# Three blocks on one core: retention's values computed tokens-major from x, half-width convolution taps that run on, and block 2's outputs in another order

## The chip, the cores and the metric

The kernel runs on 1 core of one Trainium2 chip. The metric is the device time of one execution in microseconds (us), the median of several runs; lower is better. A profile of one execution gives the span and the instructions of each engine: PE (TensorE matmuls, with PEld its weight loads), DVE (VectorE), ACT (ScalarE), POOL (GpSimd) and SP (SyncE, which only issues transfers).

## The reference, cut to what is touched

The program is three transformer-like blocks over 1024 tokens of width 1024. Only the second is changed:

```python
proj = u @ w_in[l]                       # 1024 x 7168
conv_a, conv_bp, conv_gate = ...         # 1024 columns each
q, k, v = ...                            # 4 heads x 256 columns each
ret_gate = proj[..., o6:]
a = conv_a * jax.nn.sigmoid(conv_bp)
a = _causal_depthwise_conv(a, conv_w[l], conv_b[l])        # 31 taps
a = jax.nn.silu(_layernorm(a, conv_ln_g[l], conv_ln_b[l]))
y_conv = (a @ conv_pw[l]) * jax.nn.silu(conv_gate)
q = _rotary(q); k = _rotary(k) * (RET_QK_DIM ** -0.5)
r = _retention_chunkwise(q, k, v)                          # chunks of 128 tokens
r = _head_groupnorm(r, ret_gn_g[l], ret_gn_b[l])
y_ret = r * jax.nn.silu(ret_gate)
y = jnp.concatenate([y_conv, y_ret], axis=-1) @ w_out[l]
h = h + gate * y
```

## The kernel before

All is float32. A product of full accuracy is made of three TensorE products: each operand is split into a high and a low part (`split`, L159 on ACT for the high part and L160 on DVE, or on POOL, for the low part), and high x high, high x low and low x high are added up in PSUM. `mm3` (L234 to L236) does that with a weight tile stationary and 512 tokens moving, so its result is channels-major: 128 channels on the partitions, tokens along the row.

Block 2's first stage, the *mixed stage*, goes over a list `plan` of groups. A group is 256 output columns of `w_in` (two tiles of 128) for all 1024 tokens. It is computed with seven half-size products in place of eight (`Mixed`, L638 to L640: 7 x 4 x 3 = 84 products of 512 columns), of which POOL makes the combinations of the weights (L607 to L615) and, from the third group on, also the seven low parts; ACT and DVE gather the results from PSUM (L650 to L659). There are 24 groups: 4 gates, 8 for the convolution's input (`conv`), and 4 each for q, k and v. q and k are turned by the rotary tables on DVE and POOL (L1210 to L1215). A group of v comes out channels-major, though the retention wants tokens on the partitions, so `values` transposes it on PE (16 transposes a group, L1223) and stores it in DRAM.

Behind the products stands a background queue, `core.bg`. `worked` adds `rate` x products / 16 to a counter and `tick` takes one job for each whole unit. In the mixed stage the jobs are the 31 taps of the convolution, on DVE, one instruction of 128x1024 for each tap and channel tile, with a sum of 1024 columns in PSUM (two banks). At the end of the stage `core.drain()` runs what is left.

Then comes the retention: 16 steps (4 heads x 4 pairs of chunks), each a chain of small products over PE, DVE, ACT and POOL, with `fill(n)` between its links: n pieces of the products for `conv_gate`, whose results go to DRAM. The layer norm of the convolution (sum, mean, `ln_center`, `ln_rstd`, `ln_scale`) is the background work there.

Last the outputs: the normed convolution is split into X; `w_pw` products give the convolution's output G; then `w_out` times G, while the retention's output is read back and split into X; and `block2_out` adds `w_out` times X. The tables of block 3 (`s5_tables`, 22 jobs, most of them DVE and POOL work) are the background there, at rate 1.5.

PSUM has eight banks. Before, `mm` has three, the taps' sum two in the mixed stage (where `mm` isn't used), `pa` two, `pb` two and `pc` one.

Of the kernel before, what the change touches and what calls it, by code (L numbers as in the profile page):

```python
# [1 line left out]

# [10 lines left out]
ALU = mybir.AluOpType  # L13
# [19 lines left out]
RQ = 6  # L33
RT = 8
# [3 lines left out]
RB = 13  # L38
# [19 lines left out]
class Core:  # L58


    def __init__(self, ctx, tc, ins):
# [12 lines left out]

        self.lent = ctx.enter_context(ExitStack())
        self.banks()
# [19 lines left out]
    def banks(self, name="psum_mm"):  # L96

        self.lent.close()
        self.psm = self.lent.enter_context(self.tc.tile_pool(name=name, bufs=1, space=PSUM))
# [967 lines left out]
def block2_input(core, X, h, rrb, scratch):  # L1067
# [13 lines left out]
             for i in range(RH) for n, kind in enumerate(("q", "k", "v"))]  # L1081
    order = plan[:2] + conv[:2]
    for i in range(2, KT):
        order += conv[i:i + 1] + heads[2 * i - 4:2 * i - 2]
# [48 lines left out]
def block2(core, X, scratch, tabs, keep, after):  # L1133
# [7 lines left out]
    with ExitStack() as st:  # L1141
        cvp = st.enter_context(tc.tile_pool(name="b2_conv", bufs=1, reuse_waits="tile"))
        A = [cvp.tile([P, PAD + S], F32, tag=f"a{c}", name=f"cv_{c}") for c in range(KT)]

        def tap(c, j, state):
            def run():
                if j == 0:
                    state["acc"] = core.psum("acc", (P, S))
                    nc.vector.tensor_scalar(state["acc"], A[c][:, :S], core.vec("conv_w_2", c),
                                            core.vec("conv_b_2", c), ALU.mult, ALU.add)  # L1150
                    return
                out = A[c][:, PAD:] if j == CW - 1 else state["acc"]
                nc.vector.scalar_tensor_tensor(out, A[c][:, j:j + S], core.vec("conv_w_2", j * KT + c), state["acc"],  # L1153
                                               ALU.mult, ALU.add)
            return run
# [3 lines left out]
        core.banks("psum_conv")  # L1159
        with tc.tile_pool(name="b2_mix", bufs=1, reuse_waits="tile") as pool:  # L1160
# [5 lines left out]
            turns = []  # L1166
# [4 lines left out]
            def gather(f, name):  # L1171
# [16 lines left out]
                elif name == "a22":  # L1188
                    {"conv": conv, "q": turned, "k": turned, "v": values}[kind](kind, i, g, u)
                if name in ("a12", "s2"):  # L1190
                    while turns and len(turns) > (2 if name == "a12" else 0):
                        turns.pop(0)()
# [5 lines left out]
            def conv(_, c, a, b):  # L1198
# [4 lines left out]
                core.bg += [tap(c, j, state) for j in range(CW)]  # L1203
# [14 lines left out]

            def values(_, i, a, b):
                def turn(k, y, half):  # L1220
                    pt = core.psum("pc")
                    for j in range(4):
                        nc.tensor.transpose(pt[:, j * P:(j + 1) * P], y[:, (half * 4 + j) * P:(half * 4 + j + 1) * P], core.ident)  # L1223
                    t = temp()
                    nc.scalar.activation(t, pt, AF.Copy)
                    nc.sync.dma_start(heads["v"][i, :, half * 4:half * 4 + 4, k], t.rearrange("p (b c) -> p b c", b=4))
                turns.extend([lambda k=k, y=y, half=half: turn(k, y, half) for k, y in enumerate((a, b)) for half in range(2)])
# [26 lines left out]
            while turns:  # L1254
                turns.pop(0)()
            core.paced = None
            core.drain()
        scratch["mixed"].close()
        core.banks()
        with tc.tile_pool(name="b2_ret", bufs=1, reuse_waits="tile") as pool:  # L1260
            ln = {}

            def ln_sum(c):
                if c == 0:
                    return
                if c == 1:
                    ln["acc"] = pool.tile([P, S], F32, tag="lnacc", name="ln_acc")
                nc.gpsimd.tensor_tensor(ln["acc"], A[0][:, PAD:] if c == 1 else ln["acc"], A[c][:, PAD:], ALU.add)

            def ln_mean():  # L1270
                ln["mu"] = pool.tile([P, S], F32, tag="lnmu", name="ln_mu")
# [5 lines left out]
            def ln_center(c):  # L1277
                a = A[c][:, PAD:]
                nc.vector.tensor_tensor(a, a, ln["mu"], ALU.subtract)
                if c == 0:  # L1280
                    ln["var"] = pool.tile([P, S], F32, tag="lnacc", name="ln_var")
                    nc.scalar.activation(ln["var"], a, AF.Square)
                else:
                    sq = core.raw()
                    nc.scalar.activation(sq, a, AF.Square)
                    nc.gpsimd.tensor_tensor(ln["var"], ln["var"], sq, ALU.add)

            def ln_rstd():
                ln["r"] = core.rsqrt(core.token_sums(ln["var"], pool), pool)

            def ln_rows():
                ln["r"] = core.rows(ln["r"], pool)

            def ln_spread():
                ln["rb"] = core.over_partitions(ln["r"], pool, tag="lnmu")
# [6 lines left out]
            om = pool.tile([P, P], F32, tag="onesm", name="onesm")  # L1302
            nc.vector.memset(om, 1.0 / D)
            done = list(ready)

            def ln_ready(c):
                ln_sum(c)

# [3 lines left out]
            core.bg += pause * 4 + [ln_mean] + pause * 4 + [lambda c=c: ln_center(c) for c in range(KT)]  # L1312
            core.bg += pause * 8 + [ln_rstd] + pause * 2 + [ln_rows] + pause * 2 + [ln_spread] + [lambda c=c: ln_scale(c) for c in range(KT)]
# [7 lines left out]
            def conv_gates():  # L1321
                nxt = core.weights(w_in, 0, KT, 2 * D)
                for c in range(KT):
                    w = nxt
                    for half in range(2):
                        ps = core.psum("mm")
                        for k in range(KT):
# [1292 lines left out]
```

## Time and profile before

| | before |
|---|---|
| median of 3 runs | 3751.67 us (3744.95 to 3754.52) |
| the profiled execution | 3755.68 us, its span 3753.9 us |
| busy share of the span | PE 92%, DVE 68%, POOL 48%, ACT 42% |
| mean granted clock of TensorE | 0.956 |

In the profiled execution the mixed stage goes from 1538 to 2126 us, the retention to about 2345, the two outputs that the change swaps to about 2552, and `block2_out` to 2655. A busy PE in these views is modelled: each product is shown with its whole way through the array, so that products that follow each other overlap, and the distance from start to start is what one costs in a row of them.

### The profile page before, as it was taken

Reading aid. Unit: us, or ns where it says so; the run is one execution under the profiler, and the core shown is the slowest. Engines: PE = TensorE matmul, PEld = TensorE weight load, DVE = VectorE, ACT = ScalarE, POOL = GpSimd, SP = SyncE. Lnnn points to the kernel's source line nnn. Section 1 sums busy time; section 2 is a strip of 40 time slices with the busy share of each in tenths; the row PEclk is TensorE's granted clock in tenths of the full one; section 3 lists DMA queues with packets and bytes.
Section 4 is the critical chain, followed back from the end, with each engine's and each line's share of the span. In section 5 each row is a group of like instructions: output and inputs, shape, how many; then the busy total and the mean of one; then the engine's idle time right before and its main releaser. Section 6 shows DMA issues by size and latency. Waiting matters only on the chain. (4 is left out here: it accounts for less than half of the span.)

```text
span 3753.9 us, 45804 instructions
## 1 busy us (share of the span) xinstructions
PE 3448.4 (92%) x16540; PEld 2779.9 (74%) x16540; DVE 2553.3 (68%) x3211; ACT 1571.2 (42%) x2731; POOL 1806.0 (48%) x1690
## 2 busy tenths in 40 slices
PE   8999989899998999898889989889899689899998
PEld 7878777677776778576667778668677468677876
DVE  7888897777766555768989664874556365755644
ACT  5666674433334444532223343214443124653334
POOL 2343343456554534567677653436428884331122
PEclk9999999999999999899989999999899899899999
DMA  4101026333325323322122454465443135225513
GB/s 142 37 30 37 28 69 234 109 95 107 107 93 184 114 76 120 111 73 79 62 73 68 141 160 124 126 195 185 128 152 108 57 89 159 88 84 191 178 48 110
DMA packets 431134, 409.85 MB, mean 109 GB/s; under 512 B 34059, under 2 KB 364347, under 8 KB 430907
## 3 DMA queue, kind: packets, MB, share of 16 engines
q1 hardware_dynamic: 396164, 330.27, 28.5%
q0 software_dynamic: 21088, 68.19, 5.0%
q10 hardware_dynamic: 13655, 8.46, 0.8%
q8 instruction: 131, 2.15, 0.2%
q14 instruction: 96, 0.79, 0.1%
HBM read 284.80 MB, written 122.03 MB: 108 GB/s over the span
## 5 line engine op out<-in xcount | busy, mean ns | idle before, releaser
L159 ACT ACTIVATE whi<-raw 128x512 fp32r<-128x512 f32 (+3 forms) x610 | 431.1, 737 | 787.8 <-PE pb L639 214.4
L160 DVE TENSOR_TENSOR wlo<-raw,whi 128x512 fp32r<-128x512 f32 (+3 forms) x456 | 545.9, 1219 | 227.5 <-ACT whi L159 223.9
L234 PE MATMUL mm<-x,whi 128*128 128x512 f32 x1152 | 462.4, 402 | 9.3 <-ACT whi L159 3.9
L236 PE MATMUL mm<-x,wlo 128*128 128x512 f32 x1152 | 458.0, 399 | 6.0 <-DVE wlo L160 6.0
L235 PE MATMUL mm<-x,whi 128*128 128x512 f32 x1152 | 460.4, 400 | 0.5 <-DVE x L163 0.2
L493 POOL TENSOR_TENSOR s<-s,f 128x127 f32<-128x127 f32 (+1 forms) x192 | 194.4, 1020 | 293.6 <-DVE f L492 190.9
L1153 DVE SCALAR_TENSOR_TENSOR acc<-cv,par,acc 128x1024 f32<-128x1024 f32 x232 | 298.1, 1285 | 4.3
L638 PE MATMUL pa<-x,whi 128*128 128x512 f32 x648 | 262.2, 405 | 24.2 <-ACT u L659 16.8
L234 PE MATMUL mm<-yc,whi 128*128 128x512 f32 (+1 forms) x656 | 267.1, 407 | 7.4 <-ACT whi L159 4.3
L235 PE MATMUL mm<-yc,whi 128*128 128x512 f32 (+1 forms) x656 | 266.9, 407 | 6.0 <-DVE yc L160 5.9
L640 PE MATMUL pa<-x,wlo 128*128 128x512 f32 x648 | 260.7, 403 | 8.0 <-DVE wlo L160 7.9
L236 PE MATMUL mm<-yc,wlo 128*128 128x512 f32 (+1 forms) x656 | 265.3, 405 | 1.6 <-DVE wlo L160 1.5
L639 PE MATMUL pa<-x,whi 128*128 128x512 f32 x648 | 260.5, 402 | 6.8 <-DVE x L160 6.8
L640 PE MATMUL pb<-x,wlo 128*128 128x512 f32 x576 | 234.0, 411 | 32.0 <-POOL wlo L160 22.4
L638 PE MATMUL pb<-x,whi 128*128 128x512 f32 x576 | 237.2, 412 | 27.6 <-ACT whi L159 8.8
L234 PEld LDWEIGHTS mm<-x,whi 128*128 128x128 f32 x1152 | 219.7, 191 | 56.0 <-ACT whi L159 4.7
L236 PEld LDWEIGHTS mm<-x,wlo 128*128 128x128 f32 x1152 | 218.9, 190 | 52.8 <-DVE wlo L160 7.5
L160 POOL TENSOR_TENSOR wlo<-raw,whi 128x512 fp32r<-128x512 f32 x154 | 215.4, 1418 | 82.6 <-ACT whi L159 82.5
L235 PEld LDWEIGHTS mm<-x,whi 128*128 128x128 f32 x1152 | 219.5, 191 | 45.2 <-DVE x L163 0.6
L639 PE MATMUL pb<-x,whi 128*128 128x512 f32 x576 | 234.6, 407 | 3.2 <-DVE x L160 3.1
L492 DVE TENSOR_TENSOR_SCAN f<-f 128x128 f32<-128x128 f32 (+1 forms) x192 | 196.0, 1035 | 39.7 <-ACT f L485 38.6
L607 POOL TENSOR_TENSOR raw<-raw 128x512 f32<-128x512 f32 x58 | 79.9, 1377 | 246.9 <-DMA raw<-in_ffn_w_in_dram 119.7
(599 smaller groups left out, 8443.4 us busy)
## 6 DMA issues: line engine op xcount, KB each, us to landing
raw<-in_w_in_dram SPq DMA_DIRECT2D x96, 512.0 KB
raw<-in_ffn_w_in_dram SPq DMA_DIRECT2D x44, 512.0 KB
raw<-in_w_out_dram SPq DMA_DIRECT2D x32, 512.0 KB
g<-g_dram SPq DMA_DIRECT2D x56, 256.0 KB
raw<-in_sb_w_in_dram SPq DMA_DIRECT2D x24, 512.0 KB
raw<-in_ada_w_dram SPq DMA_DIRECT2D x24, 512.0 KB
raw<-h_dram SPq DMA_DIRECT2D x18, 512.0 KB
g_dram<-t POOLq DMA_DIRECT2D x8, 1024.0 KB, 4.7
```

The costliest lines, as they stand in the source:

```text
L159: nc.scalar.activation(hi, src, AF.Copy)
L160: return (eng or nc.vector).tensor_tensor(lo, src, hi.bitcast(F32), ALU.subtract).ins
L234: nc.tensor.matmul(ps, w_h, x[:, 0, sl], start=start and k == 0, stop=False)
L235: nc.tensor.matmul(ps, w_h, x[:, 1, sl], start=False, stop=False)
L236: self.last = nc.tensor.matmul(ps, w_l, x[:, 0, sl], start=False, stop=stop and k == n - 1).ins
L492: nc.vector.tensor_tensor_scan(rev, rev, rev, 1.0, ALU.mult, ALU.bypass)
L493: nc.gpsimd.tensor_tensor(s[:, :m - 1], s[:, :m - 1], f[:, 1:m], ALU.mult)
L607: self.eng.tensor_tensor(at["s1"], at["a21"], at["a22"], ALU.add)
L638: nc.tensor.matmul(ps, hi[:, i], x[i][:, 0], start=first and i == 0, stop=False, skip_group_check=more)
L639: nc.tensor.matmul(ps, hi[:, i], x[i][:, 1], start=False, stop=False, skip_group_check=more)
L640: self.core.last = nc.tensor.matmul(ps, lo[:, i], x[i][:, 0], start=False, stop=i == self.N - 1, skip_group_check=more).ins
L1153: nc.vector.scalar_tensor_tensor(out, A[c][:, j:j + S], core.vec("conv_w_2", j * KT + c), state["acc"], ALU.mult, ALU.add)
```

## The change

- The v groups leave `plan` (20 groups stay). `values(hd)` in the retention stage now makes v tokens-major: 128 tokens of X are the stationary operand, 256 columns of weights move, three products for each of 8 row tiles and 8 token blocks, 192 products of 256 columns a head. Head 0's come before the first step, the others are `fill` pieces mixed with those of `conv_gate`. The transposes are gone.
- A tap is two instructions of 128x512, second half of the tokens first, with a sum in one bank (`cv`). `core.drain()` after the mixed stage is gone: the taps run on behind the retention and into the output. The rates are now RT 10, RQ 9 and RB 14.
- `mm` has two banks, in the whole program, since banks are no longer lent out.
- The retention's half of `w_out` comes first, and behind it the layer norm from `ln_center` on, at rate RY = 7; then `w_pw` with the normed convolution split into tiles of its own, with the tables behind it at RS = 2.5; `block2_out` then takes the convolution's half of `w_out`.

```diff
-RQ = 6
-RT = 8
+RQ = 9
+RT = 10
+RY = 7
+RS = 2.5
-RB = 13
+RB = 14
...
     def psum(self, tag, shape=(P, HALF)):
-        pool, bufs = {"mm": (self.psm, 3), "acc": (self.psm, 1), "pa": (self.ps, 2), "pb": (self.ps, 2), "pc": (self.ps, 1)}[tag]
-        return pool.tile(list(shape), F32, tag=tag, name=self.nm(tag), bufs=bufs)
+        bufs = {"mm": 2, "cv": 1, "pa": 2, "pb": 2, "pc": 1}[tag]
+        return self.ps.tile(list(shape), F32, tag=tag, name=self.nm(tag), bufs=bufs)
...
-             for i in range(RH) for n, kind in enumerate(("q", "k", "v"))]
+             for i in range(RH) for n, kind in enumerate(("q", "k"))]
...
-        def tap(c, j, state):
+        def tap(c, j, half, state):
             def run():
+                at = PAD - CW + 1 + j + half * HALF
                 if j == 0:
-                    state["acc"] = core.psum("acc", (P, S))
+                    state["acc"] = core.psum("cv")
...
-                core.bg += [tap(c, j, state) for j in range(CW)]
+                core.bg += [tap(c, j, half, state) for half in (1, 0) for j in range(CW)]
...
-            core.paced = None
-            core.drain()
         scratch["mixed"].close()
...
+            def values(hd):
+                wv = [pool.tile([P, KT, 2 * P], R32, tag=f"wv{i}", name=core.nm("wv")) for i in range(2)]
+                for i in range(2):
+                    raw = core.raw().rearrange("p (k c) -> p k c", c=P)
+                    col = 5 * D + (2 * hd + i) * P
+                    nc.sync.dma_start(raw, w_in[:, col:col + P].rearrange("(k p) c -> p k c", p=P))
+                    core.split(*(t[:, :, i * P:(i + 1) * P] for t in wv), raw)
+                yield
+                for b in range(NB):
+                    ps, bs = core.psum("mm")[:, :2 * P], slice(b * P, (b + 1) * P)
+                    for k in range(KT):
+                        for part, w in ((0, 0), (1, 0), (0, 1)):
+                            core.last = nc.tensor.matmul(ps, X[k][:, part, bs], wv[w][:, k], start=k == 0 and part + w == 0,
+                                                         stop=k == KT - 1 and w == 1).ins
+                        if k == KT - 1:
+                            t = pool.tile([P, 2 * P], F32, tag="vt", name=core.nm("vt"), bufs=2)
+                            nc.scalar.activation(t, ps, AF.Copy)
+                            nc.sync.dma_start(heads["v"][hd, :, b], t.rearrange("p (k c) -> p k c", k=2))
+                        if k % 2:
+                            core.worked(1)
+                            yield
+            def fillers():
+                gates = conv_gates()
+                for hd in range(1, RH):
+                    yield from values(hd)
+                    yield from itertools.islice(gates, 24 if hd < 3 else 0)
+                yield from gates
...
+        wts = core.weights(w_out, D, KT, 0)
+        for c in range(KT):
+            raw = core.raw()
+            nc.sync.dma_start(raw, yret[c])
+            core.split(X[c][:, 0, :], X[c][:, 1, :], raw)
...
+        core.bg += lnjobs
+        core.rate = RY
+        for m in range(KT):
...
+            if m == KT - 2:
+                core.rate = RS
...
+        while len(conv) < KT:
+            core.bg.pop(0)()
+        for m in range(KT):
+            wts = core.weights(w_pw, 0, KT, m * P)
...
```

**DVE in the mixed stage, before:** taps (`acc<-cv,par,acc`) stand between the gather's additions (`u<-u,pb`, `g<-g,pa`).

```order
L1153 SCALAR_TENSOR_TENSOR acc_13960<-cv_13213,par,acc_13960 128x1024 x3
L1201 TENSOR_TENSOR cv_13215<-g_14210,u_14272 128x1024
L1153 SCALAR_TENSOR_TENSOR acc_13960<-cv_13213,par,acc_13960 128x1024 x2
L1153 SCALAR_TENSOR_TENSOR cv_13213<-cv_13213,par,acc_13960 128x1024
L1149 TENSOR_SCALAR acc_14351<-cv_13214,par 128x1024
L650 TENSOR_TENSOR u_14413<-u_14413,pb_14338 128x512
L1153 SCALAR_TENSOR_TENSOR acc_14351<-cv_13214,par,acc_14351 128x1024 x2
L650 TENSOR_TENSOR g_14353<-g_14353,pa_14398 128x512
L1153 SCALAR_TENSOR_TENSOR acc_14351<-cv_13214,par,acc_14351 128x1024 x6
```

The same engine and stage after (a convolution group, then the start of a q group):

```order
L645 TENSOR_TENSOR u_15062<-u_15062,pb_14984 128x512
L1152 SCALAR_TENSOR_TENSOR cv_15041<-cv_13217,par,cv_15041 128x512 x3
L645 TENSOR_TENSOR g_14999<-g_14999,pa_15046 128x512
L1152 SCALAR_TENSOR_TENSOR cv_15041<-cv_13217,par,cv_15041 128x512 x4
L1195 TENSOR_TENSOR cv_13233<-g_14999,u_15062 128x1024
L1152 SCALAR_TENSOR_TENSOR cv_15041<-cv_13217,par,cv_15041 128x512
L645 TENSOR_TENSOR g_15144<-g_15144,pa_15150 128x512
```

The taps between two additions are about as many, and each has half the columns.

**PE at the end of the mixed stage, after** (`pb_16057<-t_5` is a product of the last group; `wv` and `x` are the values' weights and X, `q`, `k` the retention's first step):

```order
L635 MATMUL pb_16057<-t_5_13071,wlo_16186 128x512
L1344 MATMUL mm_16254<-wv_16244,x_6577 128x256 x2
L1344 MATMUL mm_16284<-wv_16244,x_6577 128x256 x2
L1394 MATMUL pa_16521<-q_16505,k_16506 128x128 x4
L1402 MATMUL pb_16528<-ident,k_16506 128x128 x4
L1344 MATMUL mm_16254<-wv_16245,x_6577 128x256
L1344 MATMUL mm_16254<-wv_16244,x_6578 128x256 x2
L1344 MATMUL mm_16254<-wv_16245,x_6578 128x256
```

The values' products follow the last group directly, where before the retention's own products and those of `conv_gate` stood.

**DVE in the output, after** (`raw<-mm,mod,raw` empties a bank of `mm` for `w_out`; `wlo` is the low part of the next weights; `cv<-cv,ln_mu` is `ln_center`):

```order
L1493 SCALAR_TENSOR_TENSOR raw_19029<-mm_19033,mod,raw_19029 128x512
L1259 TENSOR_TENSOR cv_13209<-cv_13209,ln_mu 128x1024
L1259 TENSOR_TENSOR cv_13213<-cv_13213,ln_mu 128x1024
L1259 TENSOR_TENSOR cv_13217<-cv_13217,ln_mu 128x1024
L1259 TENSOR_TENSOR cv_13221<-cv_13221,ln_mu 128x1024
L1259 TENSOR_TENSOR cv_13225<-cv_13225,ln_mu 128x1024
L1259 TENSOR_TENSOR cv_13229<-cv_13229,ln_mu 128x1024
L1259 TENSOR_TENSOR cv_13233<-cv_13233,ln_mu 128x1024
L1259 TENSOR_TENSOR cv_13237<-cv_13237,ln_mu 128x1024
L155 TENSOR_TENSOR wlo_19199<-raw_19196,whi_19198 128x1024
L1493 SCALAR_TENSOR_TENSOR raw_19115<-mm_19118,mod,raw_19115 128x512
```

Before, these eight stood among the retention's small instructions; now they stand ahead of a weight split and of an emptying of `mm`.

## Rows read from the trace of the kernel before

**Rows 1.** The page's head and busy line.
```profile
span 3753.9 us, 45804 instructions
PE 3448.4 (92%) x16540; PEld 2779.9 (74%) x16540; DVE 2553.3 (68%) x3211; ACT 1571.2 (42%) x2731; POOL 1806.0 (48%) x1690
```

**Rows 2.** Windows: stage, its us, busy us of PE, PEld, DVE, ACT, POOL, clock.
```profile
1688.40:2126.40 438.00, 389.19 (x1602) 305.26 (x1601) 390.90 (x351) 129.88 (x226) 322.12 (x232) 0.95 0.24 75
2126.40:2345.50 219.10, 208.67 (x1052) 177.19 (x1051) 116.67 (x223) 87.66 (x132) 93.59 (x94) 0.97 0.49 152
2345.50:2552.00 206.50, 181.51 (x1013) 143.74 (x1013) 155.14 (x279) 41.78 (x57) 71.93 (x32) 0.93 0.55 169
```

**Rows 3.** PE's waits in the mixed stretch, 1688 to 2126 us: total, times, longest.
```profile
PE pb L640 <- POOL wlo L160: 27.4, 16, 5.0
PE pa L638 <- ACT u L659: 14.6, 5, 5.6
```

**Rows 4.** DVE by line, the same stretch: count, busy us, mean ns.
```profile
L1153 DVE SCALAR_TENSOR_TENSOR acc<-cv,par,acc 128x1024 f32<-128x1024 f32 x203 | 260.8, 1285 | 3.7
L650 DVE TENSOR_TENSOR g<-g,pa 128x512 f32<-128x512 f32 x36 | 24.6, 682 | 22.2 <-PE pa L640 19.2 <-issue 2.9
...
L1153 DVE SCALAR_TENSOR_TENSOR cv<-cv,par,acc 128x1024 f32<-128x1024 f32 x8 | 10.2, 1278 | 0.2
L1149 DVE TENSOR_SCALAR acc<-cv,par 128x1024 f32<-128x1024 f32 x7 | 9.4, 1345 | 0.2
```

**Rows 5.** PE by line, the same stretch.
```profile
L638 PE MATMUL pa<-x,whi 128*128 128x512 f32 x216 | 89.5, 414 | 14.6 <-ACT u L659 14.6
...
L638 PE MATMUL pb<-t,whi 128*128 128x512 f32 x217 | 86.3, 398 | 0.0
...
L638 PE MATMUL pb<-x,whi 128*128 128x512 f32 x71 | 32.4, 457 | 6.4 <-ACT whi L159 6.2
```

**Rows 6.** POOL by line, the same stretch.
```profile
L160 POOL TENSOR_TENSOR wlo<-raw,whi 128x512 fp32r<-128x512 f32 x124 | 175.5, 1435 | 73.7 <-ACT whi L159 73.6
...
L609 POOL TENSOR_TENSOR raw<-raw,raw 128x512 f32<-128x512 f32 x18 | 24.3, 1352 | 0.7
```

**Rows 7.** Timeline of PE in an unbroken run of 512-column products: start us, us.
```profile
1400.10 0.40 PE L236 MATMUL mm<-x,wlo 128*128 128x512 f32 x1
...
1402.43 0.40 PE L234 MATMUL mm<-x,whi 128*128 128x512 f32 x1
```

**Rows 8.** Timeline of PE in block 1's attention: 256-column products of split operands.
```profile
144.70 0.29 PE L547 MATMUL pc<-ah,v 128*128 128x256 f32 x1
...
145.42 0.34 PE L479 MATMUL pa<-kh,qs 128*128 128x384 f32 x1
```

**Rows 9.** Timeline of PE in the retention: 256-column products of unsplit operands.
```profile
2160.18 1.03 PE L1388 MATMUL pc<-rstate,q 128*128 128x256 f32 x4
2161.05 0.27 PE L1367 MATMUL pa<-q,k 128*128 128x128 f32 x1
```

**Rows 10.** Weight loads by line: mean ns behind the busy us.
```profile
L547 PEld LDWEIGHTS pc<-ah,v 128*128 128x128 f32 x320 | 62.9, 197 | 6.9 <-DVE o L552 4.5 <-ACT ah L159 0.2
```

**Rows 11.** DVE by line in the retention, 2126 to 2345 us.
```profile
L1397 DVE SCALAR_TENSOR_TENSOR rstate<-rstate,pa 128x512 f32<-128x512 f32 x24 | 16.3, 679 | 17.3 <-PE pa L1392 15.8 <-PE pc L1388 1.3
...
L160 DVE TENSOR_TENSOR wlo<-raw,whi 128x1024 fp32r<-128x1024 f32 x10 | 15.7, 1571 | 15.6 <-ACT whi L159 14.7 <-PE pc L1385 0.9
```

**Rows 12.** DVE by line in the outputs, 2345 to 2552 us.
```profile
L1474 DVE SCALAR_TENSOR_TENSOR raw<-mm,mod,raw 128x512 f32<-128x512 f32 x16 | 11.9, 746 | 10.6 <-PE mm L236 10.6
```

**Rows 13.** Timeline of PE: first product into an `mm` tile, in block 1, in block 3.
```profile
240.95 0.39 PE L234 MATMUL mm<-x,whi 128*128 128x512 f32 x1
...
3176.72 0.39 PE L234 MATMUL mm<-yc,whi 128*128 128x512 f32 x1
```

**Rows 14.** Timeline of DVE: reading of the `mm` tile two before, at these places.
```profile
268.32 0.66 DVE L376 TENSOR_TENSOR t<-mm,rbc_mix 128x512 f32<-128x512 f32 x1
...
3187.91 0.69 DVE L2071 TENSOR_TENSOR xc<-mm,rrb 128x512 f32<-128x512 f32 x1
```

More of the change, by code (lines that the diff above doesn't have):

```diff
@@ L1188, in gather @@
                 elif name == "a22":
[L1189 to L1192, printed above, removed]
+                    {"conv": conv, "q": turned, "k": turned}[kind](kind, i, g, u)
             def gate(i, k, y, rest):
@@ L1217, in turned @@
                 nc.sync.dma_start(heads[kind][i, :, 1], b)
[L1219 to L1227, printed above, removed]
             ready = []
@@ L1311, in block2 @@
             core.bg += [lambda c=c: ln_sum(c) for c in range(len(done), KT)]
[L1312 to L1313 removed]
+            core.bg += pause * 4 + [ln_mean]
+            lnjobs += [lambda c=c: ln_center(c) for c in range(KT)]
+            lnjobs += pause * 2 + [ln_rstd] + pause * 2 + [ln_rows] + pause * 2 + [ln_spread]
+            lnjobs += [lambda c=c: ln_scale(c) for c in range(KT)] + [lambda c=c: ln_split(c) for c in range(KT)[::-1]]
+            lnjobs += [tables]
             core.rate = RB
@@ L1323, in conv_gates @@
                 for c in range(KT):
[L1324 to L1327, printed above, removed]
-                            core.mm3(ps, w, X[k:k + 1], half, k0=k, start=k == 0, stop=k == KT - 1)
-                            if k == KT - 1:
-                                t = pool.tile([P, HALF], F32, tag="t", name=core.nm("cg"), bufs=2)
-                                nc.scalar.activation(t, ps, AF.Silu)
-                                nc.gpsimd.dma_start(sgate[c][:, hs(half)], t)
-                            if half == 1 and k == 0 and c + 1 < KT:
-                                nxt = core.weights(w_in, 0, KT, 2 * D + (c + 1) * P)
-                            yield
@@ L1337, in block2 @@
-            gates = conv_gates()
+                    w, ps = nxt, {}
+                    order = [(half, k) for half in range(2) for k in range(KT)]
+                    if c == KT - 1:
+                        order = [(half, k) for k in range(KT) for half in range(2)]
+                    for n, (half, k) in enumerate(order):
+                        if k == 0:
+                            ps[half] = core.psum("mm")
+                        core.mm3(ps[half], w, X[k:k + 1], half, k0=k, start=k == 0, stop=k == KT - 1)
+                        if k == KT - 1:
+                            t = pool.tile([P, HALF], F32, tag="t", name=core.nm("cg"), bufs=2)
+                            nc.scalar.activation(t, ps[half], AF.Silu)
+                            nc.gpsimd.dma_start(sgate[c][:, hs(half)], t)
+                        if n == KT and c + 1 < KT:
+                            nxt = core.weights(w_in, 0, KT, 2 * D + (c + 1) * P)
+                        yield
@@ L1339, in fill @@
+            def fillers():
[4 more added lines that the diff above has]
+                yield from gates
+            work = fillers()
             def fill(n):
                 for _ in range(n):
-                    next(gates, None)
+                    next(work, None)
+            for _ in values(0):
+                pass
             steps = [(hd, c2) for hd in range(RH) for c2 in range(NB // 2)]
```

140 lines of the change are left out of this document (67 added, 73 removed).

## The prediction

> **What bounds the kernel now.** The page comes first: PE is busy for 92% of the span, DVE for 68% [rows 1]. So only idle time of PE can be won, and only where there is some. The windows show where block 2 has it, in three stretches [rows 2]. In the mixed stretch (438.0 us) DVE is busy for 390.9 us, 89%, the highest share of the three; POOL has 322.1 us. In the retention DVE has 116.7 of 219.1 us, in the outputs 155.1 of 206.5: over both 271.8 of 425.6, 64%. Work is unevenly spread, and the change spreads it.
>
> What PE needs in the mixed stretch is worked out from its lines: 216 + 217 + 71 = 504 first products, three times that is 1512, and 84 make a group, so these are 18 groups [rows 5]. In an unbroken run ten 512-column products take from 1400.10 to 1402.43 us, 0.233 us each [rows 7], so a group needs 19.6 us. It takes 438.0 / 18 = 24.3 us. PE's named waits there are for low parts that POOL makes (27.4 us) and for a copy by ACT (14.6 us) [rows 3], and neither engine is full. The full one is DVE: 390.9 / 18 = 21.7 us a group, of which taps are 260.8 + 10.2 + 9.4 = 280.4 us, 218 of them at about 1.285 us [rows 4]. I read it so: DVE sets the pace, and the group takes 2.6 us more than DVE's own work since its queue also holds the gather's additions, which must empty the banks for PE.
>
> **The mixed stretch after.** Four of the 18 groups, those of v, leave it. For the other 14 I add up each engine.
> PE: 19.6 us a group.
> DVE: the rest without taps is 390.9 - 280.4 = 110.5 us; the four groups take 12 additions of 0.682 us with them [rows 4], which leaves 102.3. Each of the seven products of a group adds rate x 4 / 16 to the counter, so a group has 17.5 ticks at RT 10 and 15.75 at RQ 9; with 7 groups of q and k and 7 others that is 233 half taps. No row shows a half tap. Its lower bound is half of 1.285 us, 0.643; its upper one the 128x512 instruction of the same operation that adds from PSUM in the outputs, 0.746 [rows 12]; the nearest is the same operation in the retention, with its sum in PSUM and nothing beside it, 0.679 [rows 11], and that I take: 158 us (150 to 174). Together 260 us, 18.6 a group (18.0 to 19.7), against 21.7 before.
> POOL: 322.1 less 28 splits of 1.435 us and 16 combinations of some 1.352 us [rows 6] is 260 us, 18.6 a group.
> So no engine is ahead of PE any more, but three stand within one us of each other and still wait in turn. The group then takes between PE's 19.6 us, if nothing is left of the waiting, and today's 24.3. I take PE's need and two thirds of today's 2.6 us: 21.4, or 14 x 21.4 = 300 us (274 to 340). Saved: 438 - 300 = **138 us** (98 to 164). The 64 transposes are in the 438.
>
> **What comes into the retention.** 4 x 192 = 768 products of 256 columns, on PE alone, with a weight load each. The nearest row is the attention's: also 256 columns, also split operands, also a load before each; six of them go from 144.70 to 145.42 us, 0.12 us each [rows 8]. The retention's own 256-column products cost (2161.05 - 2160.18) / 4 = 0.22 us [rows 9], but their operands aren't split, and this is the upper bound. I take 0.12: 768 x 0.12 = **92 us** (to 169). It lies on the path, since PE is 95% busy in that stretch. What it does for the steps' chain (more filling between the links) I count as nothing: PE is already filled there.
>
> The eight splits of the values' weights (1.571 us each, 12.6 us [rows 11]) and the taps that run on go to DVE. 283 ticks are spent when the mixed stage ends, so some 215 half taps are left, 146 us. DVE's load after the mixed stage is then 271.8 + 146 + 12.6 = 430 us in 425.6 + 92 = 518 us, 83%. That isn't over the brim, but the cover is thinner: PE isn't busy in 35.4 of the 425.6 us at 64% (8%), and in 48.8 of the 438.0 at 89% (11%) [rows 2]. On that line 83% costs about 2.5% of 518 us more: **13 us** (0 to 25). It would be seen in the outputs: `ln_center` and `ln_scale` are eight instructions in a row there, ahead of the next weights' low part and of an emptying of `mm`.
>
> **Priced at nothing.** The swap of the outputs as such: the same products in another order, and one more place where PE passes from one X to the next. For it speaks that the first output's products go tile by tile as X is split. `mm` with two banks is a rival, below.
>
> **The sum.** 3755.7 (the profiled execution) - 138 + 92 + 13 = 3723. That execution lies 4.0 us above the median of the runs shown, so on their footing **3719 us**, 0.9% less. Less than 0.3%, 11 us, can't be told from no change here.
>
> **The rivals.**
> (1) *The groups stay at 24.3 us.* If it isn't DVE but the chain from combination to split on ACT and POOL that sets the pace, the lighter taps help nothing: PE's longest sum of waits is for POOL's low parts [rows 3], and q and k, which load POOL most, are now 7 of 14 groups and no longer 7 of 18. Then 98 is saved, not 138: 3755.7 - 98 + 92 + 13 - 4 = 3759, no change. Against it: POOL is busy for 74% there and idles 73.7 us for ACT [rows 6].
> (2) *Better.* The groups fall to PE's 19.6 us and the later stretches lose nothing: 3755.7 - 164 + 92 - 4 = 3680.
> (3) *Slower: two banks for `mm`.* Wherever today the third tile is begun before the first has been read, PE must wait or do other work. In block 1 a third tile is begun at 240.95 us and the tile two before is read at 268.32 [rows 13, 14]; in block 3 the two stand at 3176.72 and 3187.91. In block 1 other work can be pulled ahead; at most the third tile's 24 products (5.6 us) lose their place in each of the 8 head pairs, 45 us. With the 11.2 us of block 3 that is 56, and 3719 + 56 = 3775. It is slower by over 0.3% once such waits cost 33 + 11 = 44 us. Against it: the reading at 268 is late because nobody waits for it, not since DVE couldn't.
> (4) *Slower: loads are not hidden.* If a product must wait until its own weights are in, a 256-column product costs 0.12 us and its load of 0.197 us [rows 10], 0.32 in all: 768 x 0.32 = 243 us and not 92, hence 3870. Rows 8 speak against it: six loads and six products in 0.72 us. The Trainium skill has this rule (TensorE: Matmul & The Clock Gate, The mechanism): weight loads overlap running products only when their row groups differ, which full 128-row tiles never do. By that rule this change would lose; the trace disagrees, with 0.12 us from product to product.
>
> **How the numbers follow.** Forecast (3690 to 3740): 0.58. Better: 0.12. No gain: 0.17. Two banks: 0.10. Loads not hidden: 0.03. Faster by over 0.3% are the first two, 0.70; within it the third, 0.17; slower the last two, 0.13. The range 3685 to 3760 leaves out most of the last two and about half of the second, under 2 in 10. The forecast's own range is the 3690 to 3740.
>
> **What would show each step.** Right: the mixed stage's 20 groups end some 130 to 140 us earlier, with PE's start-to-start of the v products at 0.12 us and half taps at 0.64 to 0.75; DVE at 80 to 90% in all three stretches; retention about 90 us longer. Wrong: groups still over 23 us (rival 1); in block 1 or 3 a span longer by tens of us and PE waiting for readers of `mm` (rival 3); v products 0.2 us and more apart (rival 4); or, in the outputs, a PE that waits for `wlo` or for the emptying of `mm` behind the layer norm and the tables for more than 25 us over today's.

## The result, and the profile after

The changed kernel takes 3771.75 us (median of 5 runs, 3766.79 to 3778.33), the kernel before 3750.94 us on the same chip: ratio 1.0058, 95% interval 1.0044 to 1.0073. It is 0.6% slower; 0.9% faster was forecast, and 3771.75 lies above the range. The profiled execution took 3771.72 us, its span is 15.7 us longer than before's [rows 1]. The page's head and busy line after:

```profile
span 3769.6 us, 46732 instructions
PE 3460.8 (92%) x16908; PEld 2806.1 (74%) x16908; DVE 2620.0 (70%) x3447; ACT 1563.3 (41%) x2705; POOL 1760.1 (47%) x1646
```

Windows after: the mixed stage's first six groups, its other 14, the retention, the three outputs in their order (retention's half of `w_out`, `w_pw`, block 2's last output), and the first two of block 3's three parts. The columns are those of [rows 2]: behind the busy times stand the granted clock (1.00 is full speed), the share of the DMA engines and GB/s.

```profile
1544.30:1686.50 142.20, 126.26 (x510) 98.35 (x510) 99.81 (x126) 61.59 (x106) 94.87 (x67) 0.93 0.24 74
1686.50:2022.60 336.10, 293.01 (x1178) 230.70 (x1176) 295.17 (x353) 99.54 (x169) 266.49 (x190) 0.94 0.24 78
2022.60:2295.30 272.70, 271.19 (x1697) 246.46 (x1698) 232.32 (x388) 75.98 (x129) 64.94 (x80) 0.99 0.45 140
2295.30:2414.00 118.70, 102.62 (x438) 82.68 (x437) 78.39 (x71) 42.81 (x45) 29.90 (x20) 0.91 0.41 134
2414.00:2524.00 110.00, 102.49 (x556) 80.39 (x554) 94.22 (x226) 21.67 (x32) 51.51 (x19) 0.97 0.50 136
2524.00:2641.60 117.60, 103.30 (x548) 82.81 (x547) 79.98 (x70) 50.78 (x80) 76.01 (x55) 0.91 0.54 169
2641.60:3186.00 544.40, 475.14 (x2309) 379.18 (x2308) 305.24 (x388) 189.70 (x294) 341.21 (x543) 0.93 0.39 115
3186.00:3396.70 210.70, 192.14 (x1099) 149.69 (x1097) 132.55 (x198) 117.44 (x206) 69.96 (x51) 0.93 0.26 83
```

The windows of before at the same places (its outputs in the order `w_pw`, convolution's half of `w_out`, last output; its 18 groups are in [rows 2]):

```profile
1538.00:1688.40 150.40, 130.64 (x505) 99.27 (x504) 108.01 (x118) 68.44 (x116) 96.80 (x67) 0.90 0.22 70
...
2126.40:2310.50 184.10, 173.67 (x885) 147.65 (x884) 100.93 (x182) 77.22 (x115) 84.34 (x82) 0.96 0.52 165
2310.50:2433.60 123.10, 109.56 (x612) 88.82 (x610) 87.06 (x234) 27.56 (x44) 43.78 (x24) 0.94 0.43 117
2433.60:2550.30 116.70, 105.25 (x565) 83.04 (x564) 82.40 (x83) 23.67 (x32) 36.91 (x19) 0.94 0.63 200
2550.30:2637.30 87.00, 87.00 (x385) 72.06 (x384) 39.52 (x40) 45.31 (x70) 66.11 (x51) 1.00 0.52 168
2637.30:3185.20 547.90, 480.76 (x2334) 382.34 (x2333) 307.89 (x388) 188.60 (x294) 338.95 (x542) 0.93 0.39 115
3185.20:3376.50 191.30, 177.06 (x1059) 138.38 (x1058) 124.10 (x193) 113.72 (x201) 69.03 (x50) 0.94 0.26 82
```

Subtracting one from the other gives the ledger:

| stage | before | after | difference | predicted |
|---|---|---|---|---|
| ahead of the mixed stage | 1538.0 | 1544.3 | +6.3 | 0 |
| first six groups | 150.4 | 142.2 | -8.2 | 0 |
| the other groups (18, then 14) | 438.0 | 336.1 | -101.9 | -138 |
| retention | 184.1 | 272.7 | +88.6 | +92 |
| `w_pw`, and one half of `w_out` | 239.8 | 228.7 | -11.1 | together with the next row +13 |
| last output | 87.0 | 117.6 | +30.6 | |
| block 3 | 1116.6 | 1128.0 | +11.4 | 0 |

Two rows carry the result: the groups, which fell from 24.3 to only 336.1 / 14 = 24.0 us, and the last output. (The first two rows move against each other; the section on the banks comes back to them.) The last 6.1 us of the 336.1 belong to no group. The values' products follow the last group in order, but not at once, since PE waits for the split of their weights:

```profile
PE mm L1344 <- ACT wv L154: 6.1, 1, 6.1
```

Without this wait the groups took 330.0 / 14 = 23.6 us. DVE's own work per group was to fall from 21.7 to 18.6 us and fell to 295.17 / 14 = 21.1. DVE by line in the 14 groups after (busy us, mean ns), taps and one of the four rotary lines:

```profile
L1152 DVE SCALAR_TENSOR_TENSOR cv<-cv,par,cv 128x512 f32<-128x512 f32 x224 | 168.2, 751 | 4.4
...
L1209 DVE TENSOR_TENSOR u<-u,cos 128x512 f32<-128x512 f32 x16 | 19.0, 1187 | 0.0
...
L1148 DVE TENSOR_SCALAR cv<-cv,par 128x512 f32<-128x512 f32 x8 | 6.4, 804 | 0.1
```

The same rotary line before, in its 18 groups:

```profile
L1214 DVE TENSOR_TENSOR u<-u,cos 128x512 f32<-128x512 f32 x16 | 12.6, 787 | 0.0
```

The taps take 168.2 + 6.4 = 174.6 us where 158 was forecast; the rotary's 62 instructions on DVE, as many as before, take 84.5 us in all where they took 71.0. So this profile alone still fits "DVE sets the pace", with a DVE that is 88% busy; only experiments can tell. Waits in the 14 groups after (who waits, for whom: total us, times, longest):

```profile
PE pb L635 <- POOL wlo L155: 31.0, 14, 3.6
...
POOL wlo L155 <- ACT whi L154: 36.3, 15, 4.9
...
ACT u L654 <- DMA q_dram<-u: 30.4, 4, 8.7
ACT u L654 <- DMA k_dram<-u: 24.6, 4, 8.1
```

Read from the top: PE waits for POOL's low parts, POOL for ACT's high parts, and ACT 55.0 us in 8 pieces for the store of a tile `u`. The timeline of ACT in the group behind a q group, after, shows one of the eight (in brackets the idle time ahead and what ended it):

```profile
1787.86 1.15 ACT L154 ACTIVATE whi<-raw 128x512 fp32r<-128x512 f32 x2 [1.52 <-PE pa L634]
1797.69 0.60 ACT L654 ACTIVATE u<-pa 128x512 f32<-128x512 f32 x1 [8.68 <-DMA q_dram<-u]
1799.05 0.63 ACT L1194 ACTIVATE u<-u 128x512 f32<-128x512 f32 x1 [0.75 <-DVE u L645]
1799.58 0.58 ACT L648 ACTIVATE g<-pb 128x512 f32<-128x512 f32 x1
1802.06 1.15 ACT L154 ACTIVATE whi<-raw 128x512 fp32r<-128x512 f32 x2 [1.89 <-PE pa L634]
```

There is one buffer of `u`. The next group's copy into it stands in ACT's queue, must wait until the rotated `u` lies in DRAM, and behind it stand the high parts of the weights: none is made between 1789 and 1802 us.

### The profile page after: what moved, and what is told of

It is laid out like the page before. It is cut to its first block, busy times and chain, and to the rows that moved or that the text cites. A ratio compares the mean times of both kernels' runs of the same rounds, so it can differ in the third digit from the quotient of the medians.

```text
span 3769.6 us, 46732 instructions
## 1 busy us (share of the span) xinstructions
PE 3460.8 (92%) x16908; PEld 2806.1 (74%) x16908; DVE 2620.0 (70%) x3447; ACT 1563.3 (41%) x2705; POOL 1760.1 (47%) x1646
## 4 chain that ended last, share of the span: by engine, by line
PE 57%; POOL 13%; DVE 13%; DMA 8%; issue 6%; ACT 3%; SPq 0%; POOLq 0%; ACTq 0%; DVEq 0%
PE mm L229 9%; PE mm L230 9%; PE mm L231 9%; DVE wlo L155 3%; POOL wlo L155 3%; PE pb L635 3%; PE pb L633 3%; PE pb L634 3%; POOL sc L1896 2%; PE pa L633 2%; PE pa L635 2%; PE pa L634 2%; DMA raw<-in_w_in_dram 2%; PE mm L1344 2%; POOL s_H L1897 2%
## 5 line engine op out<-in xcount | busy, mean ns | idle before, releaser
L154 ACT ACTIVATE whi<-raw 128x512 fp32r<-128x512 f32 (+3 forms) x582 | 413.9, 742 | 786.6 <-PE pb L634 196.6
L155 DVE TENSOR_TENSOR wlo<-raw,whi 128x512 fp32r<-128x512 f32 (+3 forms) x456 | 561.3, 1252 | 209.0 <-ACT whi L154 206.2
L1152 DVE SCALAR_TENSOR_TENSOR cv<-cv,par,cv 128x512 f32<-128x512 f32 x480 | 360.7, 751 | 10.2
L488 POOL TENSOR_TENSOR s<-s,f 128x127 f32<-128x127 f32 (+1 forms) x192 | 211.0, 1110 | 292.9 <-DVE f L487 149.8
L633 PE MATMUL pa<-x,whi 128*128 128x512 f32 x600 | 239.9, 400 | 13.6 <-ACT whi L154 7.1
L633 PE MATMUL pb<-x,whi 128*128 128x512 f32 x560 | 229.5, 410 | 22.1 <-ACT g L652 6.6
L635 PE MATMUL pa<-x,wlo 128*128 128x512 f32 x600 | 239.1, 399 | 9.1 <-DVE wlo L155 9.1
L634 PE MATMUL pa<-x,whi 128*128 128x512 f32 x600 | 238.8, 398 | 7.2 <-DVE x L155 7.2
L634 PE MATMUL pb<-x,whi 128*128 128x512 f32 x560 | 226.9, 405 | 0.0
L229 PE MATMUL mm<-yc,whi 128*128 128x512 f32 (+1 forms) x528 | 215.9, 409 | 11.1 <-DVE xc L2104 7.3
L231 PE MATMUL mm<-yc,wlo 128*128 128x512 f32 (+1 forms) x528 | 214.6, 407 | 1.2 <-DVE wlo L155 1.2
L230 PE MATMUL mm<-yc,whi 128*128 128x512 f32 (+1 forms) x528 | 215.6, 408 | 0.0
L155 POOL TENSOR_TENSOR wlo<-raw,whi 128x512 fp32r<-128x512 f32 x126 | 183.6, 1479 | 41.1 <-ACT whi L154 41.1
```

The source lines that it names most:

```text
L154: nc.scalar.activation(hi, src, AF.Copy)
L155: return (eng or nc.vector).tensor_tensor(lo, src, hi.bitcast(F32), ALU.subtract).ins
L229: nc.tensor.matmul(ps, w_h, x[:, 0, sl], start=start and k == 0, stop=False)
L230: nc.tensor.matmul(ps, w_h, x[:, 1, sl], start=False, stop=False)
L231: self.last = nc.tensor.matmul(ps, w_l, x[:, 0, sl], start=False, stop=stop and k == n - 1).ins
L488: nc.gpsimd.tensor_tensor(s[:, :m - 1], s[:, :m - 1], f[:, 1:m], ALU.mult)
```

## The experiments

All are timed against the kernel before, which took 3752 to 3754 us as the median of each set of runs. A name with b_ is an edit of the kernel before, one with a_ or u2_ an edit of the changed kernel.

### What sets the pace of the groups

**b_fewtaps**, before with 2 of the 31 taps:

```diff
-                core.bg += [tap(c, j, state) for j in range(CW)]
+                core.bg += [tap(c, j, state) for j in (0, CW - 1)]
```

> The kernel before, which leaves out 29 of the 31 taps of the convolution. Theory of the prediction, 'DVE sets the pace of the mixed groups': DVE's share there falls from 89% to about 30%, the 18 groups of the stretch fall from 24.3 to about 20 us each, the stretch from 438 to about 360. Rival 'another chain sets the pace' (ACT and POOL, which prepare the weights): the groups stay above 22.5 us although DVE idles most of the time.

3742.63 us, ratio 0.9980 (0.9970 to 0.9991). Its window over the same 18 groups:

```profile
1689.90:2126.40 436.50, 391.26 (x1599) 308.69 (x1598) 159.92 (x144) 130.68 (x227) 322.84 (x232) 0.93 0.24 75
```

DVE is busy for 159.92 of the 436.50 us, 37%, and the group still takes 436.5 / 18 = 24.3 us. The prediction's theory, that DVE's load holds the groups at 24 us, fell here.

**a_u2**, the changed kernel with a second buffer:

```diff
-                    at[f, "u"] = tp.tile([P, S], F32, tag="u", name=core.nm("u"), bufs=1)
+                    at[f, "u"] = tp.tile([P, S], F32, tag="u", name=core.nm("u"), bufs=2)
```

> The changed kernel with one edit: the tile u, into which the groups gather, has two buffers in place of one. Theory 'u holds ACT': in the changed kernel ACT waits 55 us in 8 pieces for the store of a q or k group's u, its queue then holds back the high parts, POOL the low parts, and PE waits. With a second buffer the groups that follow a q or k group fall from 25 to 28 us to about 20, the 14 groups from 336 to about 290 us, and the kernel to about 3730 us. Rival 'DVE or POOL sets the pace' (88% and 79% busy): the wait only moves, the 14 groups stay above 325 us and the kernel at 3765 or more.

3735.62 us, ratio 0.9952 (0.9937 to 0.9968), 36.1 us less than the changed kernel. Its window of the 14 groups, and the two waits that answer to those above:

```profile
1687.60:1987.50 299.90, 278.32 (x1178) 221.58 (x1177) 289.59 (x351) 98.94 (x169) 268.51 (x190) 0.98 0.27 87
```
```profile
PE pb L635 <- POOL wlo L155: 4.8, 7, 1.4
...
POOL wlo L155 <- ACT whi L154: 1.2, 5, 0.3
```

The groups take 299.9 / 14 = 21.4 us, with DVE at 97%. That this is the forecast's figure is chance, since it was to come from lighter taps, and without the wait for the values' weights (6.0 us here) it is 21.0. The stretch gives 336.1 - 299.9 = 36.2 us, as much as the two medians differ. So a DVE at 37% left the groups at 24.3 us, and one at 97% let them fall to 21.4: its share said nothing about the pace of 24. Whether DVE costs any of the time that is left above PE's 19.6 isn't shown. Its own work is 289.59 / 14 = 20.7 us a group there, PE's named waits are now 6.9 us for its additions into `u` and 8.4 for POOL's low parts, and no run has both a second buffer and fewer taps.

**b_u2**, before with the same edit:

> The kernel before with one edit: the tile u has two buffers. Theory 'u holds ACT': in before ACT waits 17 us for stores of u, a fifth of what it did in the changed kernel with one buffer (55 us) and PE's waits named for u are 14.6 us, so the gain is smaller than the 36 us there: the 18 groups fall from 438 to some 415 us, the kernel to about 3730 us. If in before the wait of ACT lies in one queue with the waits for g and for the transposes, it may be as much as 40 us (3710). Rival 'DVE sets the pace': no change. The difference to the changed kernel with two buffers (3735.6) is then what the change itself is worth without this wait.

3709.96 us, ratio 0.9884 (0.9870 to 0.9898), 44 us less than before, at the upper end of what was expected. The 18 groups:

```profile
1687.40:2066.60 379.20, 362.63 (x1577) 292.35 (x1576) 361.15 (x332) 130.11 (x226) 325.13 (x232) 0.99 0.27 86
```

They fall from 438.0 to 379.2 us, 21.1 each, where 415 was expected; 11.9 us of that are lost again in one wait of PE for the read of k at the start of the retention:

```profile
2078.97 2.05 PE L1367 MATMUL pa<-q,k 128*128 128x128 f32 x8 [11.88 <-DMA k<-k_dram]
```

So the one buffer set the pace before the change too. Named waits for `u`'s store were smaller there than after (17 against 55 us, nearly a third and not a fifth), yet the gain is larger: the length of one named wait was a poor measure of what the buffer costs.

With two buffers on both sides, the change makes the kernel 3735.62 - 3709.96 = 26 us slower, so something else costs too. In the two profiled executions, 23.0 us apart, the changed kernel is 79.3 us shorter in the groups, 62.6 longer from there to the end of the second output, 31.8 longer in the last output (118.8 against 87.0, the length of before) and 7.7 longer in block 3.

### The last output

**u2_ry14** and **a_ry14**, the changed kernel with two buffers of `u` and with one, each with the layer norm at twice the rate:

```diff
-RY = 7
+RY = 14
```

> The changed kernel with two buffers of u, and RY 14 in place of 7: the layer norm starts and ends earlier in the retention's half of w_out, so the tables do too; on DVE their last instructions stand three emptyings ahead of block 2's last output and no longer one. Theory 'the end of the tables costs': the waits for hr in the last output (10.8 us) shrink by half or more and the kernel takes 5 to 10 us less than 3735.6. Rival: the clusters of the norm cost more instead, no change.

> The changed kernel as it is (one buffer of u) with RY 14 in place of 7. Theory 'late tables': the 37 us that RY 14 gave beside the second buffer of u are its own, since the two lie in different stages: about 3735 us, block 2's last output at some 92 us and no longer 118. Rival 'the two only work together': over 3755.

3698.45 us (0.9859, 0.9841 to 0.9877) and 3741.02 us (0.9961, 0.9947 to 0.9975): 37 and 31 us less than with RY 7. The second is near what was expected; for the first only 5 to 10 us were, so the waits for `hr` alone were a poor measure again. The outputs of a_ry14 in the same three windows:

```profile
2291.20:2401.60 110.40, 102.00 (x442) 81.22 (x441) 79.82 (x101) 42.92 (x45) 31.39 (x20) 0.95 0.49 147
2401.60:2520.00 118.40, 108.44 (x625) 82.89 (x625) 103.59 (x209) 23.73 (x37) 59.93 (x24) 0.94 0.50 141
2520.00:2612.40 92.40, 91.60 (x474) 75.56 (x473) 57.52 (x55) 46.41 (x71) 66.08 (x48) 1.00 0.58 184
```

The last output falls from 117.6 to 92.4 us, at a granted clock of 1.00, full speed, in place of 0.91, and all three from 346.3 to 321.2. The other 6 us of the gain lie in stages that the edit doesn't touch. What costs is thus the tables' end, which RY 7 lets run into the last output: ACT's last copies for the tables end at 2545 us before, ahead of that output, and at 2569 in the changed kernel, 45 us into it. The layer norm must end before they start. The next run moves the tables the other way.

**u2_lnpaced**, two buffers of `u`, the layer norm's jobs spread:

```diff
-            lnjobs += [lambda c=c: ln_center(c) for c in range(KT)]
+            lnjobs += [j for c in range(KT) for j in (lambda c=c: ln_center(c), pause[0])]
...
-                nc.vector.scalar_tensor_tensor(hr[:, hs(half)], ps[half], ...)
+                core.paced = nc.vector.scalar_tensor_tensor(hr[:, hs(half)], ps[half], ...).ins
```

> The changed kernel with two buffers of u; in addition the layer norm's jobs are spread: an empty job behind each ln_center and ln_scale, and each waits for the last emptying of mm, so that 4, 2, 2 and 6, 1, 1 of them stand in a row on DVE and no longer 8 and 8. Theory 'the clusters cost': the waits of 5.6 and 7.6 us in the retention's half of w_out shrink to under 3 us, 8 to 12 us less than 3735.6. Rival 'the time comes back': the norm ends later, the tables start later, their end reaches further into the next output, and the gain there is lost: within 4 us of 3735.6.

3739.70 us (0.9961, 0.9949 to 0.9974), no gain against 3735.62: the rival held. The first and the last of its three outputs, and below them those of a_u2:

```profile
2259.40:2371.70 112.30, 100.46 (x437) 79.97 (x435) 77.22 (x70) 41.94 (x44) 30.21 (x21) 0.95 0.44 141
...
2470.20:2605.20 135.00, 107.37 (x605) 84.53 (x604) 91.22 (x88) 49.89 (x79) 84.47 (x56) 0.85 0.53 165
```
```profile
2261.60:2381.00 119.40, 102.21 (x438) 82.18 (x437) 79.26 (x71) 42.85 (x45) 29.91 (x20) 0.91 0.41 134
...
2489.90:2608.70 118.80, 102.14 (x547) 81.99 (x546) 81.19 (x74) 50.94 (x80) 74.40 (x55) 0.91 0.55 171
```

The clusters' waits shrink (119.4 us in a_u2 become 112.3), the tables come later still, and the last output grows from 118.8 us in a_u2 to 135.0.

**u2_noln**, two buffers of `u`, and on DVE `ln_center` and `ln_scale` are left out:

```diff
-                nc.vector.tensor_tensor(a, a, ln["mu"], ALU.subtract)
...
-                nc.vector.tensor_tensor(a, a, ln["rb"], ALU.mult)
```

> The changed kernel with two buffers of u; it leaves out the 16 instructions of ln_center and ln_scale on DVE, so the convolution isn't normed. A price for the clusters of 8: if they cost what the chain of waits shows in the retention's half of w_out (5.6 and 7.6 us and what the clock loses), 13 to 18 us less than 3735.6; if the tables, which then start earlier, also matter, over 20.

3723.18 us (0.9916, 0.9902 to 0.9929), 12 us less than a_u2, just under the smaller of the two figures. Its first output takes 107.3 us in place of a_u2's 119.4, its last 111.8 in place of 118.8, the one between 4.3 more. So the clusters cost about 12 us or less, since the tables start earlier too.

**a_subdve**, the changed kernel with one line of the last output moved from POOL to DVE:

```diff
-        sub = lambda out, a, b: nc.gpsimd.tensor_tensor(out, a, b, ALU.subtract)
+        sub = lambda out, a, b: nc.vector.tensor_tensor(out, a, b, ALU.subtract)
```

> The changed kernel with the subtractions of block 2's last output (18 us of POOL) on DVE. In that stage two low parts of 128x1024 on DVE took 7.7 and 11.25 us, where 1.22 is usual, and ended 1.1 us behind an unbroken run of POOL instructions. Theory 'POOL's unbroken runs shut DVE out': with shorter runs the longest such instruction stays under 5 us, and the stage, 117.6 us, gets 5 to 12 us shorter, although DVE has more to do. Rival 'ACT is late behind the tables' stores and everything follows': the long instructions go, but the stage keeps its length within 4 us.

3756.11 us (1.0010, 1.0001 to 1.0019), 16 us less than the changed kernel; the stage itself goes from 117.6 to 109.5 us, 8.1 less. The rest of the gain lies behind it, in block 3, which the edit doesn't touch (1114.5 us in place of 1128.0 in the profiled executions), and isn't explained. What the edit is about stands in the two engines' timelines of the changed kernel. DVE:

```profile
2578.27 7.70 DVE L155 TENSOR_TENSOR wlo<-raw,whi 128x1024 fp32r<-128x1024 f32 x1 [3.22 <-ACT whi L154]
...
2594.33 11.25 DVE L155 TENSOR_TENSOR wlo<-raw,whi 128x1024 fp32r<-128x1024 f32 x1
```

POOL at the second of these places:

```profile
2593.97 1.31 POOL L298 TENSOR_TENSOR acc_s<-acc_s,sq 128x512 f32<-128x512 f32 x1
2595.22 0.57 POOL L1551 DMA_DIRECT2D h_dram<-hr  x1
2595.82 2.55 POOL L298 TENSOR_TENSOR acc_s<-acc_s,sq 128x512 f32<-128x512 f32 x2
2598.32 1.29 POOL L1527 TENSOR_TENSOR ts<-x,t 128x512 f32<-128x512 f32 x1
2599.57 1.27 POOL L1527 TENSOR_TENSOR ts<-x,x 128x512 f32<-128x512 f32 x1
2600.81 2.47 POOL L298 TENSOR_TENSOR acc_s<-acc_s,sq 128x512 f32<-128x512 f32 x2
2603.25 1.25 POOL L1527 TENSOR_TENSOR ts<-x,ts 128x512 f32<-128x512 f32 x1
```

DVE's instruction starts while POOL is in the first of these. POOL's run ends at 2604.50 us; DVE's instruction ends at 2605.58, 1.08 later, nearly its usual 1.2 us. At the first place POOL runs without a break from 2576.13 to 2584.88, and DVE's instruction ends at 2585.97, 1.09 later. With the subtractions on DVE its longest low part of this size in the stage is:

```profile
2603.98 1.65 DVE L155 TENSOR_TENSOR wlo<-raw,whi 128x1024 fp32r<-128x1024 f32 x1
```

And why POOL had such a backlog, from ACT's timeline of the changed kernel:

```profile
2571.33 0.63 ACT L294 ACTIVATE acc_s<-raw 128x512 f32<-128x512 f32 x1 [2.64 <-DMA tabS_dram<-sbt]
```

The last output's squares start on ACT only after the tables' last store has landed, 47 us behind the stage's first product; by the order of the pools in the kernel their sums are to lie where that store was read from. The work then comes all at once. The theory's forecast held and the rival's didn't: the shut-out is worth some 8 us of the stage. By the lines above it follows from the late tables itself, since they heap up POOL's work. The rest of the 25 us that a_ry14 takes out of this stage isn't divided further.

### The banks

**b_mm2**, before with two banks of `mm`, and **a_mm3**, the changed kernel with a third one outside of the taps' time (by before's scheme of a pool that is opened anew):

```diff
-        pool, bufs = {"mm": (self.psm, 3), ...
+        pool, bufs = {"mm": (self.psm, 2), ...
```
```diff
+        core.banks(2)
         core.rate = RT
...
         core.rate = 0
+        core.banks(3)
         st.close()
```

> The kernel before with one edit: mm has two banks for products in place of three, everywhere. Theory 'two banks cost': in the two profiles the changed kernel lost 6.3 us ahead of block 2 and 11.4 us behind it, where nothing else was changed, so this kernel is slower than before by 12 to 25 us, about half of it in block 3's stretch from 3185 to 3393 us. Rival 'the banks are free': the 17.7 us came from somewhere else (other addresses, other order), and this kernel stays within 5 us of before.

> The changed kernel with the third bank for mm in all places where the taps don't need their own: before the mixed stage, and from block 2's last output on. Theory 'two banks cost': 12 to 18 us less than the changed kernel, 3754 to 3760 us, with block 3's stretch back at about 208 us. Rival 'the banks are free': it stays at 3771 give or take 5.

3746.33 us (0.9986, 0.9976 to 0.9996) and 3772.47 us (1.0059, 1.0045 to 1.0073). Two banks alone make before no slower, the third gives the changed kernel nothing. In b_mm2 the mixed stage starts at 1544.0 us, 6 later than before, and its first six groups take 141.7 us, 8.7 less: these two rows of the ledger are the banks', and cancel. In a_mm3, with three banks there, the mixed stage starts at 1537.0 us.

**b_u2mm2**, b_u2 and b_mm2 together:

> The kernel before with two buffers of u and two banks of mm. If banks are about free or a small gain, as they were alone (5 us less), 3700 to 3710 us; then the changed kernel with two buffers of u and RY 14 (3698) is worth under 0.3% against a kernel before that has the same help.

3718.27 us (0.9905, 0.9889 to 0.9921), 8 us more than b_u2, so no small gain here.

**u2_ry14_ssd3**, u2_ry14 with the third bank from block 3's scan on:

```diff
+    core.banks(3)
     dt, a, tri, m4 = decay.dt, decay.a, decay.tri, decay.m4
```

> The changed kernel with two buffers of u and RY 14, and a third bank of mm from block 3's scan over chunks on (3119 to 3323 us there, 204 us; with three banks before it was 191). Theory 'banks cost where mm waits for its readers': that stretch takes some 192 us, and the kernel 8 to 14 us less than 3698, since the places where two banks were the shorter ones stay as they are. Rival 'what a bank gives in one stretch is lost in the next': within 5 us of 3698.

3714.02 us (0.9898, 0.9881 to 0.9914), 16 us more than u2_ry14: neither the theory nor its rival held. The stretch stays at 204.4 us, and what follows it is longer:

```profile
3123.00:3327.40 204.40, 184.05 (x1078) 143.81 (x1076) 132.07 (x192) 112.70 (x202) 69.89 (x50) 0.92 0.25 79
```

That stretch takes 191 to 194 us in the kernels that have three banks all through block 3, and 200 to 211 in the others, but a_mm3 loses elsewhere in block 3 what it wins there. Two banks in place of three make from -5 to +8 us of the whole kernel, a third one from the scan on made 16 more; no net cost of two banks is shown.

## Why the prediction was wrong

**The step that failed** is "I read it so: DVE sets the pace" of the mixed groups. DVE's 89% was the highest share of an engine, and the rest of PE's waiting was put down to its queue. b_fewtaps took that load away and the pace stayed. The pace was the one buffer of `u`: ACT's wait for it held back the high parts, those POOL's low parts, and those PE; a second one took the groups from 24.3 to 21.1 us in before and from 23.6 to 21.0 after (without the wait for the values' weights). So at that pace lighter taps were worth nothing, and only the four groups' absence counted: -101.9 us, against 98 in rival 1 and 138 in the forecast. Rival 1 had the price right and named the chain over ACT and POOL, but not what held ACT. The argument against it, that POOL idles for ACT, was the trace of the true cause.

**The values' products** were priced right. 135 of them in a row in the changed kernel:

```profile
2032.26 16.00 PE L1344 MATMUL mm<-wv,x 128*128 128x256 f32 x135
```

That is 0.12 us each, as in [rows 8]; the retention grew by 88.6 us, where 92 was forecast. Not priced was that their weights come late, the 6.1 us at the end of the groups. Rival 4 fell. By the rule quoted there from the Trainium skill (TensorE: Matmul & The Clock Gate, The mechanism) each of these, with a full tile of new weights, would have had to wait for its load; the trace disagrees a second time. The prediction quotes only half of it: that section of the Trainium skill also lets a load into a background weight buffer run ahead of products. With that the trace is in keeping, though it doesn't show such a buffer.

**The half taps** take 0.751 us on average in the changed kernel, by the same view that gave 1.285 for a whole one; 0.679 was taken, 0.746 was the upper bound, so the bound was 0.005 short. At the pace that one buffer of `u` sets it didn't matter, as b_fewtaps shows; with two it may, which no run tests.

**The outputs** are the second step that failed. The swap was priced at nothing, as the same products in another order; but it put the norm, and with it the tables' end, later, and the last output took 30.6 us more, of which an earlier norm takes 25 away (a_ry14). Beside it 13 us were charged to DVE's load, to be seen at the layer norm's clusters. (By the prediction's own two points 83% gives some 2.2% of 518 us, 11 and not 13.) That size is about right, as u2_noln shows. It is hidden in the ledger, where the retention's half of `w_out` with the clusters took only 2.0 us more than the product that stood second before, and `w_pw` 13.1 less. The prediction looked at what DVE runs, not at what is late next: the norm delays the tables, the tables block 2's last output.

**Two banks** (rival 3) were rightly kept out of the sum: b_mm2 and a_mm3 show no net cost. The +11.4 us in block 3 is not settled. It lies in the stretch from 3186 to 3397 us (+19.4, against -8.0 in the rest); there the kernels with two banks are longer, but a third bank for that stretch didn't shorten it.

**The sum.** 36 us of the 53 between 3719 and 3772 are the groups; 6.5 the outputs above their 13, less 3.4 in the retention; block 3 and what lies ahead of the 14 groups 9.5; that makes 49. The remaining 4 were taken off in the forecast for the distance from profiled execution to median, which after is nil (3771.72 and 3771.75 us). The two costs that were found can be taken away by one number each: u2_ry14 takes 3698.45 us, 1.4% less than before and the shortest here. Against b_u2 in the same set of runs (3709.96) it is 11.5 us, 0.3%, ahead. The two intervals overlap, and only the changed kernel had a rate set anew, so it isn't shown that the change is worth anything by itself.

## What to carry to other kernels

An engine that is busy for 89% of a stretch need not set its pace; leave half its work out, or follow the named wait upwards (PE for POOL, POOL for ACT, ACT for a store) to the first link that waits for a buffer. When work is moved later, ask first for what waits behind it: here the norm pushed the tables, and the tables held the space of the stage after. Spreading a cluster is no gain when its last instruction is what others wait for; running it earlier was.

## What was unexpected in the hardware

An instruction of DVE with two operands in SBUF that usually takes 1.2 us took 7.70 and 11.25 us beside unbroken runs of POOL instructions, and ended about one of its own lengths after the run. The Trainium skill (SBUF — State Buffer, SBUF: two separate sides) has it that such a DVE instruction and a POOL one that reads SBUF share a pair of ports as an exclusive lock: whichever starts first has it for its whole instruction, and the other is blocked. The rows agree that DVE is blocked, and show more: at the second place it stayed out for eight POOL instructions and an issue, from 2594.33 to 2604.50 us, not for one. This isn't the rule, though. In the mixed stage of the same kernel a smaller one of DVE, usually 0.68 us, got in behind a single instruction of POOL's unbroken run:

```profile
1786.01 1.76 DVE L1205 TENSOR_TENSOR rt<-g,sin 128x512 f32<-128x512 f32 x1 [0.53 <-POOL g L1208]
```
```profile
1785.93 1.30 POOL L1210 TENSOR_TENSOR u<-u,rt 128x512 f32<-128x512 f32 x1
1787.19 3.40 POOL L155 TENSOR_TENSOR wlo<-raw,whi 128x512 fp32r<-128x512 f32 x2
```

DVE was done at 1787.77, while POOL went on to 1790.59. What decides who comes next isn't shown.
